# W_mix_out's product: five split weight blocks kept from the first token group for the second

## The chip, the cores and the metric

One core of one Trainium2 chip runs the kernel. The metric is the device time of one launch in microseconds (us), median of the runs shown. Every figure below is of this core.

## The reference

One layer of an encoder for 1024 tokens of width 1024, in float32. Three sub-layers follow each other, each between two RMS norms; the change lies in the end of the second one:

```
x = x + 0.5 * post1(SwiGLU_1(pre1(x)))
u = pre_mix(x)
y_ret, y_na, gates = ...                              # from u @ W_mix_in: retention, neighbourhood attention
m = sigmoid(gate_ret) * y_ret + sigmoid(gate_na) * y_na
x = x + post_mix(m @ W_mix_out)                       # W_mix_out: 1024 x 1024
x = x + 0.5 * post2(SwiGLU_2(pre2(x)))
```

## The kernel before, in words

**Split products.** TensorE multiplies in a rounded float32 (`fp32r`). Each operand is therefore split: ScalarE casts the high part h (`split`, line 60, rows "CAST"), VectorE subtracts it from the source for the rest l (line 61). A product is three matmuls, h·h, h·l, l·h (`mm3`, lines 87 to 89).

**The stage.** `out_proj` multiplies m, transposed, by W_mix_out, here `wmo`: eight blocks of 128 rows (k = 0 to 7). Left of the product stands m of one k for a group of tokens, right `wmo[k]` in two halves of 512 columns. There are eight tiles of 128 tokens in three groups, (0, 1, 2), (3, 4, 5) and (6, 7), called here the first, second and third. A group of three holds two of the six PSUM banks `ps` for each token tile. A group goes through its k one by one, for all its tokens; its last three k (`tail=3`) are held together and gone through token tile by token tile, so that the first tile is done early and its epilogue can begin. In the trace a step of one matmul of 512 columns takes 0.227 us, so one k of a group of three, 18 matmuls, takes 4.1 us.

**Weights.** `load_w` loads `wmo[k]` (512 KB) with a DMA of SyncE's queue into `wraw` (four buffers) and splits it into two pairs of pieces, rings `wh` and `wl` of nine buffers each: four and a half blocks. Each of the three groups loads and splits all eight blocks again.

**Left side.** `stream` loads m of one k for the tokens of the group (`graw`, two buffers, SyncE's queue) and splits it into `gh` and `gl` (three buffers each). m comes from the stage before, which keeps it in tiles of the pool `ro` and stores each of them to DRAM by GpSimd's queue (`store`, line 67; rows "m<-m"). The pool ends with the stage, and its memory goes on to the pool `a2`.

**Epilogue of a token tile** (`Ep.__call__`): ScalarE squares the two banks with a sum (line 219), the inverse root is taken (`rstd`, line 97, GpSimd), VectorE scales and adds the residual (lines 226 and 228), the sum is stored, normed again (line 117) and transposed on TensorE (line 126, lagging by some products) into `wx`, an object of `Winograd`. That one builds the factors of X for the next product, the third sub-layer's, in 14 buffers of tag "x" of `a2`; some come only late in this stage.

**Order.** Each engine works through its own list in order. The lists are not those of the program's text: a scheduler with a model of the times places every instruction, and a load is placed once its buffer is free by that model. A wait in front of a list holds back whatever is behind it, whether it needs that or not.

The split, the two other places that the steps below name:

```
            nc.scalar.copy(h, src)                                    # L60
            (eng or nc.vector).tensor_tensor(l, src, hf, ALU.subtract)    # L61
        raw = self.wpool.tile([P, D], F32, tag="wraw", name="wraw", bufs=4)
        self.nc.sync.dma_start(raw[:, :n], src)                       # L71
```

Of the kernel before, what the change touches and what calls it, by code (L numbers as in the profile page):

```python
# [11 lines left out]
F32R = mybir.dt.float32r  # L12
# [6 lines left out]
P = 128  # L19
D = 1024  # L20
S = 1024
KT = D // P
# [15 lines left out]
class Core:  # L38
# [94 lines left out]
            ks = slice((k % 4) * P, (k % 4 + 1) * P)  # L133
            self.mm3(bank, [p[:, ks] for p in w[k // 4]], xop(k, h), k == 0, k == nk - 1)

    def out_proj(self, nk, lhs, wload, done, groups=((0, 1, 2), (3, 4, 5), (6, 7)), tail=3, lag=8, space=3):

        left = []  # L140

        def one(t, k, a, w):
            for e in [e for e in left if e[0] <= 0]:
                left.remove(e)
                f = e[1]()
                if f is not None:
                    left.append([2, f])
            for b in range(2):
                self.mm3(banks[t][b], a[t], w[b], k == 0, k == nk - 1)
            for e in left:  # L150
                e[0] -= 1

        for toks in groups:
            banks = {t: [self.bank() for _ in range(2)] for t in toks}
            tl = tail if len(toks) > 1 else 0
            for k in range(nk - tl):
                w, a = wload(k), lhs(k, toks)
                for t in toks:
                    one(t, k, a, w)
            last = [(k, lhs(k, toks), wload(k)) for k in range(nk - tl, nk)]  # L160
            for t in toks:
                for k, a, w in last:
                    one(t, k, a, w)
                f = done(t, banks[t])
                if f is not None:
                    left.append([max(lag, max([e[0] for e in left], default=-space) + space), f])
        return [f for _, f in left]
# [508 lines left out]
def stream(c, pool, src):  # L676

    def lhs(k, toks):
        n = len(toks) * P
        p0 = toks[0] * P  # L680
        raw = pool.tile([P, 384], F32, tag="graw", name="graw", bufs=2)
        h = pool.tile([P, 384], F32R, tag="gh", name="gh", bufs=3)
        l = pool.tile([P, 384], F32R, tag="gl", name="gl", bufs=3)
        c.nc.sync.dma_start(raw[:, :n], src(k)[:, p0:p0 + n])
        c.split(h[:, :n], l[:, :n], raw[:, :n])
        return {t: (h[:, j * P:(j + 1) * P], l[:, j * P:(j + 1) * P]) for j, t in enumerate(toks)}
    return lhs
# [344 lines left out]
def trunk_layer(ctx: ExitStack, tc, x, g1a, w1i, w1o, g1b, gma, wmt, wnv, wrv, logits, dtab, rope, bias,  # L1032
# [7 lines left out]
    c = Core(tc, const, wpool, psum, dram)  # L1040
# [4 lines left out]
    def dt(name, shape):  # L1045
        return dram.tile(shape, F32, name=name)
# [3 lines left out]
    x1, x2 = dt("x1", [S, D]), dt("x2", [S, D])  # L1050
    d = {
        "a21": dt("a21", [P, 4, 512]),
        "nq": dt("nq", [NHP, P, S]), "nk": dt("nk", [NHP, P, S]), "nv": dt("nv", [16, 64, 512]), "nvg": dt("nvg", [4, 4, P, 512]),
        "no": dt("no", [NHP, P, S]), "rq": dt("rq", [RH, P, S]), "rk": dt("rk", [RH, P, S]),
        "rv": dt("rv", [TT, P, D]), "rg": dt("rg", [8, P, S]), "ry": dt("ry", [8, P, S]),
        "sr": dt("sr", [8, P, S]), "sn": dt("sn", [8, P, S]), "z": dt("z", [8, P, S]), "m": dt("m", [8, P, S]),
    }

    def rows(a):
        return lambda t: a[t * P:(t + 1) * P, :]  # L1060
# [3 lines left out]
    def pool(stack, name, side="left"):  # L1064
        return stack.enter_context(tc.tile_pool(name=name, bufs=1, side=side))


    with tc.block(schedule_with_timeline_sim=True):
        apool = pool(right, "a1", "right")
        early = pool(right, "early", "right")  # L1070
        wx = Winograd(c, (apool,) * 3, early, (14,) * 7)
# [12 lines left out]
        with tc.tile_pool(name="fin1", bufs=1) as fp:  # L1084
# [8 lines left out]
        wx = Winograd(c, (x0pool, x1pool, spool), None, (4, 4, 2, 8, 8, 8, 8), d["a21"])  # L1093
        ep_stack, g_stack = ExitStack(), ExitStack()
        ep = pool(ep_stack, "ep1")
# [7 lines left out]
        rest = ffn_out(c, xt, [junk[:, i] for i in range(4)], q, Blocks(c, (g0, g1, g1, g1), (1, 3)), w1o, wf[0], gl[0], fo,  # L1103
                       {n: (lambda j=j: ahead.update({j: c.load_w(wnv[j])})) for j, n in enumerate((65, 66, 73))})
# [65 lines left out]
        with tc.tile_pool(name="pa", bufs=1) as pa:  # L1170
# [12 lines left out]
            for i, (_, _, f, g, fn) in enumerate(jobs):  # L1183
# [14 lines left out]
                if i == mx.held + mx.saved - 1:  # L1198
# [3 lines left out]
                    for k in range(2):  # L1202
                        raw = c.raw(d["a21"][:, 2 * k:2 * k + 2].rearrange("p k t -> p (k t)"))
# [81 lines left out]
    gs = pool(g_stack, "gs2", "right")  # L1285
    ro = pool(y_stack, "ro")
    for k in range(KT):
        raw = c.raw(d["ry"][k])
        c.split(yop[0][k // 4][:, k % 4], yop[1][k // 4][:, k % 4], raw)
    for i0 in (0, 3, 6):  # L1290
        tiles = range(i0, min(i0 + 3, 8))
        m, z, w, banks = {}, {}, {}, {}
# [28 lines left out]
    apool = pool(a_stack, "a2", "right")  # L1321
    cmb = pool(left, "cmb2")
    wx = Winograd(c, (apool,) * 3, cmb, (14,) * 7)
    with tc.tile_pool(name="ep2", bufs=1) as ep:
        rest = c.out_proj(KT, stream(c, gs, lambda k: d["m"][k]), lambda k: c.load_w(wmo[k]),
                          Ep(c, ep, gmb, g2a, False, rows(x1), rows(x2), wx.put))
        fin = Pairs(c, wx, [(w2i[i], w2i[FT + i]) for i in LeftFactors.order], 3, 3)
        places = []

        def save():  # L1330
            if not places:
                h, l, r = ([gs.tile([P, 384], F32, tag=n, name=n, bufs=b) for _ in range(b)]
                           for n, b in (("gh", 3), ("gl", 3), ("graw", 2)))
                for e in (h, l):
                    places.extend([[e[0], e[1][:, :128]], [e[1][:, 128:], e[2][:, :256]]])
                places.extend([[r[0], r[1][:, :128]], [r[1][:, 128:], h[2][:, 256:], l[2][:, 256:]]])
            return places.pop(0)

        fin.lead(save, rest)
        assert not places  # L1340
        for f in rest:
            f()
# [94 lines left out]
```

## Time and profile before

| | us |
|---|---|
| median of three runs (lowest, highest) | 2271.83 (2271.73, 2274.43) |
| the profiled execution: time | 2273.08 |
| the profiled execution: span of the trace | 2271.3 |
| busy: PE (matmuls) | 2211.0 |
| busy: VectorE (DVE) | 1699.6 |
| busy: ScalarE (ACT) | 1004.9 |
| busy: GpSimd (POOL) | 577.1 |
| product of W_mix_out in the trace: the first group's first matmul | 1515.88 |
| the next product's first matmul that waits | 1612.30 |

PE is the matmul engine, PEld its weight loads, DVE, ACT and POOL are VectorE, ScalarE and GpSimd, SP and SPq SyncE and its DMA queue. In a timeline a row gives the start, the duration, engine, line, operation, the tiles out<-in and the shape; in square brackets stand the idle time ahead of it and who ended it. Successive instructions overlap by a little in these rows, so the step from start to start is shorter than the duration. The granted clock of TensorE is 0.993 on average.

### The profile page before, as it was taken

What the parts mean: (1) busy time and instruction counts of PE and PEld (TensorE: products, weight loads), DVE (VectorE), ACT (ScalarE), POOL (GpSimd) and SP (SyncE); (2) the same over time, 40 slices, a digit from 0 to 9 for tenths busy, and PEclk for the clock granted to TensorE, in tenths of its full rate; (3) what the DMA queues carried; (4) which work ended last, traced back from release to release, by engine and by line L of the source; (5) the groups of instructions that cost most, each with busy time, mean ns of one, the idle gap of its engine ahead of it and who ended that gap; (6) DMA issues with size and microseconds to landing.
All of it is one profiled execution on the core that took longest, in us unless ns stands there. A gap on an engine that the chain in (4) does not pass through costs nothing.

```text
span 2271.3 us, 30229 instructions
## 1 busy us (share of the span) xinstructions
PE 2211.0 (97%) x10288; PEld 1837.1 (81%) x10288; DVE 1699.6 (75%) x2952; ACT 1004.9 (44%) x2117; POOL 577.1 (25%) x741
## 2 busy tenths in 40 slices
PE   6999999999999999989999999999899999999998
PEld 5888888878887878878888888887688888887886
DVE  7897777655879769869876678547989887875576
ACT  6332222344555222358876665326633322234453
POOL 3243434210332224311001222101114343421022
PEclk9999999999999999999999999999999999999999
DMA  5355555476754453357655566866535555547664
GB/s 192 105 170 184 186 183 186 165 271 199 236 176 144 149 194 111 135 196 245 206 163 170 163 218 228 296 211 213 177 114 188 195 189 176 185 139 237 198 234 151
DMA packets 162459, 424.72 MB, mean 187 GB/s; under 512 B 19776, under 2 KB 47552, under 8 KB 162240
## 3 DMA queue, kind: packets, MB, share of 16 engines
q1 hardware_dynamic: 121824, 289.07, 39.5%
q0 software_dynamic: 40480, 133.72, 15.9%
q8 instruction: 81, 1.33, 0.3%
q14 instruction: 74, 0.61, 0.1%
HBM read 303.70 MB, written 123.21 MB: 188 GB/s over the span
## 4 chain that ended last, share of the span: by engine, by line
PE 42%; issue 7%; DVE 4%; DMA 3%; ACT 2%; POOL 1%; SPq 0%; POOLq 0%; DVEq 0%; ACTq 0%
PE ps L87 13%; PE ps L89 13%; PE ps L88 13%; DMA wraw<-in_dram 1%; PE pt L88 1%; PE pt L87 1%; PE pt L89 1%; DVE wl L61 1%; POOL rstd L97 1%; DMA vraw<-rv 0%; ACT wh L60 0%; DVE x L538 0%; DMA sn<-ev 0%; DVE tmp L117 0%; DMA vraw<-nvg 0%
## 5 line engine op out<-in xcount | busy, mean ns | idle before, releaser
L61 DVE TENSOR_TENSOR wl<-wraw,wh 128x512 fp32r<-128x512 f32 x662 | 479.8, 748 | 88.2 <-ACT wh L60 86.1
L60 ACT CAST wh<-wraw 128x512 fp32r<-128x512 f32 x670 | 390.6, 618 | 244.8 <-PE ps L88 71.0
L87 PE MATMUL ps<-wh,gh 128*128 128x512 f32 x612 | 239.7, 395 | 6.9 <-ACT gh L60 6.1
L88 PE MATMUL ps<-wl,gh 128*128 128x512 f32 x612 | 240.6, 394 | 0.7 <-DVE wl L61 0.7
L89 PE MATMUL ps<-wh,gl 128*128 128x512 f32 x612 | 235.2, 395 | 2.0 <-DVE gl L61 2.0
L61 DVE TENSOR_TENSOR gl<-graw,gh 128x512 fp32r<-128x512 f32 (+2 forms) x178 | 130.4, 736 | 141.0 <-ACT gh L60 138.1
L60 ACT CAST gh<-graw 128x512 fp32r<-128x512 f32 (+2 forms) x178 | 106.5, 601 | 197.8 <-PE ps L88 83.0
L87 PEld LDWEIGHTS ps<-wh,gh 128*128 128x128 f32 x612 | 116.3, 190 | 33.9 <-ACT gh L60 7.8
L89 PEld LDWEIGHTS ps<-wh,gl 128*128 128x128 f32 x612 | 116.1, 191 | 28.3 <-DVE gl L61 4.5
L528 POOL TENSOR_TENSOR q<-q,gain 128x512 f32<-128x512 f32 x30 | 52.8, 1779 | 335.7 <-ACT junk L527 124.0
L88 PEld LDWEIGHTS ps<-wl,gh 128*128 128x128 f32 x612 | 116.3, 190 | 25.2 <-DVE wl L61 1.5
L60 ACT CAST wh<-t 128x512 fp32r<-128x512 f32 x58 | 36.1, 622 | 214.9 <-DVE t L386 214.9
L87 PE MATMUL ps<-a11h,wh 128*128 128x512 f32 x280 | 110.6, 395 | 1.5 <-ACT wh L60 1.5
L87 PE MATMUL ps<-a12h,wh 128*128 128x512 f32 x280 | 110.8, 396 | 0.7 <-ACT wh L60 0.6
L87 PE MATMUL ps<-a22h,wh 128*128 128x512 f32 x280 | 109.8, 392 | 0.0
L89 PE MATMUL ps<-a22h,wl 128*128 128x512 f32 x280 | 109.1, 390 | 0.5 <-DVE wl L61 0.5
L89 PE MATMUL ps<-a12h,wl 128*128 128x512 f32 x280 | 109.6, 391 | 0.0
L88 PE MATMUL ps<-a11l,wh 128*128 128x512 f32 x280 | 109.6, 391 | 0.0
L89 PE MATMUL ps<-a11h,wl 128*128 128x512 f32 x280 | 109.6, 391 | 0.0
L88 PE MATMUL ps<-a12l,wh 128*128 128x512 f32 x280 | 109.4, 391 | 0.0
L88 PE MATMUL ps<-a22l,wh 128*128 128x512 f32 x280 | 109.1, 390 | 0.0
L97 POOL TENSOR_TENSOR rstd<-ss,mhalf 128x1 f32<-128x1 f32 x80 | 59.4, 745 | 184.6 <-DVE ss L221 74.4
(365 smaller groups left out, 5946.1 us busy)
## 6 DMA issues: line engine op xcount, KB each, us to landing
wraw<-in_dram SPq DMA_DIRECT2D x247, 512.0 KB, 4.4
lead<-in_dram POOLq DMA_DIRECT2D x44, 256.0 KB, 3.8
g0s<-cmb POOLq DMA_DIRECT2D x44, 256.0 KB, 3.0
graw<-g0s SPq DMA_DIRECT2D x44, 256.0 KB, 2.7
wq<-in_dram POOLq DMA_DIRECT2D x44, 256.0 KB, 4.0
g1s<-cmb POOLq DMA_DIRECT2D x44, 256.0 KB, 3.6
graw<-g1s SPq DMA_DIRECT2D x44, 256.0 KB, 2.7
bt<-in_dram SPq DMA_DIRECT2D x24, 384.0 KB, 3.4
```

The source lines that it names most:

```text
L60: nc.scalar.copy(h, src)
L61: (eng or nc.vector).tensor_tensor(l, src, hf, ALU.subtract)
L87: mm(ps, a[0], b[0], start=start, stop=False, skip_group_check=more)
L88: mm(ps, a[0], b[1], start=False, stop=False, skip_group_check=more)
L89: mm(ps, a[1], b[0], start=False, stop=stop, skip_group_check=more)
L97: self.nc.gpsimd.tensor_tensor(r[:, :n], ms, self.mhalf[:, :n], ALU.pow)
L528: (eng or c.nc.gpsimd).tensor_tensor(h if out is None else out, h, self.post[:, b * 512:(b + 1) * 512], ALU.mult)
```

## The change

In the first group the blocks k = 3 to 7 are no longer split into `wh` and `wl`: they go to five tiles `wk`, of four times 512 columns (both halves, h and l), in buffers of tag "x", which X's later factors take when these five are done. They stay there. The second group takes k in the order 3, 4, 5, 6, 7, 0, 1, 2, the first five from `wk`, and loads and splits only 0, 1 and 2; these are now its tail. The third group loads all eight. Five loads of 512 KB, ten casts and ten subtractions go; the matmuls are as many as before.

```diff
-    def out_proj(self, nk, lhs, wload, done, groups=((0, 1, 2), (3, 4, 5), (6, 7)), tail=3, lag=8, space=3):
+    def out_proj(self, nk, lhs, wload, done, groups=((0, 1, 2), (3, 4, 5), (6, 7)), tail=3, lag=8, space=3, orders=()):
...
-                self.mm3(banks[t][b], a[t], w[b], k == 0, k == nk - 1)
+                self.mm3(banks[t][b], a[t], w[b], k == ends[0], k == ends[1])
...
-        for toks in groups:
+        for n, toks in enumerate(groups):
             banks = {t: [self.bank() for _ in range(2)] for t in toks}
             tl = tail if len(toks) > 1 else 0
-            for k in range(nk - tl):
+            ks = orders[n] if n < len(orders) else range(nk)
+            ends = ks[0], ks[-1]
+            for k in ks[:nk - tl]:
                 w, a = wload(k), lhs(k, toks)
                 for t in toks:
                     one(t, k, a, w)
-            last = [(k, lhs(k, toks), wload(k)) for k in range(nk - tl, nk)]
+            last = [(k, lhs(k, toks), wload(k)) for k in ks[nk - tl:]]
...
     with tc.tile_pool(name="ep2", bufs=1) as ep:
-        rest = c.out_proj(KT, stream(c, gs, lambda k: d["m"][k]), lambda k: c.load_w(wmo[k]),
-                          Ep(c, ep, gmb, g2a, False, rows(x1), rows(x2), wx.put))
+        kept, asked = {}, []
+
+        def wload(k):
+            asked.append(k)
+            if asked.count(k) == 2 and k in kept:
+                return kept.pop(k)
+            if asked.count(k) > 1 or k < 3:
+                return c.load_w(wmo[k])
+            raw = c.raw(wmo[k])
+            w = apool.tile([P, 4, 512], F32R, tag="x", name="wk", bufs=14)
+            kept[k] = [(w[:, b], w[:, 2 + b]) for b in range(2)]
+            for b in range(2):
+                c.split(*kept[k][b], raw[:, b * 512:(b + 1) * 512])
+            return kept[k]
+
+        rest = c.out_proj(KT, stream(c, gs, lambda k: d["m"][k]), wload,
+                          Ep(c, ep, gmb, g2a, False, rows(x1), rows(x2), wx.put), orders=(range(KT), (*range(3, KT), *range(3))))
```

Lines behind 150 stand two further down in the changed kernel (219 is 221, 684 is 686). The order of the instructions around the first group, on the engine that splits, ScalarE, from the last stage's end to the first epilogue. Before (`wh` is a weight piece, `gh` the left side of one k for the group, `ps` a bank):

```order
L60 CAST wh<-wraw 128x512 x8
L60 CAST gh<-graw 128x384
L60 CAST wh<-wraw 128x512 x2
L60 CAST gh<-graw 128x384
L60 CAST wh<-wraw 128x512
L219 ACTIVATE tmp,ss_15335<-ps 128x512 x2
```

The two rows "gh" and "wh x2" repeat up to the last left side, k = 7, which is followed by one more weight cast and the first epilogue. The same place after the change:

```order
L60 CAST wh<-wraw 128x512 x4
L60 CAST gh<-graw 128x384
L60 CAST wk<-wraw 128x512 x5
L60 CAST gh<-graw 128x384
L60 CAST wk<-wraw 128x512 x5
L60 CAST gh<-graw 128x384
L60 CAST wh<-wraw 128x512 x5
L60 CAST gh<-graw 128x384
L60 CAST wh<-wraw 128x512 x4
L60 CAST gh<-graw 128x384
L221 ACTIVATE tmp,ss_15320<-ps 128x512 x2
```

The ten casts of the blocks that are kept now stand as a run behind the left sides of k = 3 and 4. Behind them come, still in the first group, nine casts of pieces that belong to later groups (six for k = 0, 1, 2 of the second, three for the third), five ahead of the left side of k = 6 and four ahead of that of k = 7. Before, two weight casts stood between one left side and the next.

SyncE's queue at the same place, before (`gpost`, `gpre` and `epx` belong to the epilogue):

```order
L71 DMA wraw<-in_dram 128x1024 x3
L205 DMA gpost<-in_dram 128x1024
L209 DMA gpre<-in_dram 128x1024
L215 DMA epx<-x_100 128x1024 x2
L684 DMA graw<-m 128x384
L71 DMA wraw<-in_dram 128x1024 x2
L684 DMA graw<-m 128x384
L71 DMA wraw<-in_dram 128x1024
L684 DMA graw<-m 128x384
L71 DMA wraw<-in_dram 128x1024
```

After:

```order
L71 DMA wraw<-in_dram 128x1024 x2
L207 DMA gpost<-in_dram 128x1024
L211 DMA gpre<-in_dram 128x1024
L217 DMA epx<-x_100 128x1024 x2
L686 DMA graw<-m 128x384
L71 DMA wraw<-in_dram 128x1024 x2
L686 DMA graw<-m 128x384
L71 DMA wraw<-in_dram 128x1024 x2
L686 DMA graw<-m 128x384
L71 DMA wraw<-in_dram 128x1024 x2
```

Between two loads of the left side now stand two weight loads instead of one: the loads of later groups come earlier. TensorE's order is the same but for the names of the weights, and from the third group's first epilogue on every engine's order is that of before.

## Prediction

> **What bounds the kernel now.** I read the page's busy shares first, then the stage in slices of 20 us, then the waits ahead of TensorE's instructions there, last the lists of the engines that feed it. On the page:
>
> ```profile
> span 2271.3 us, 30229 instructions
> PE 2211.0 (97%) x10288; PEld 1837.1 (81%) x10288; DVE 1699.6 (75%) x2952; ACT 1004.9 (44%) x2117; POOL 577.1 (25%) x741
> ```
>
> TensorE is busy for 97% of the span. VectorE and ScalarE, which the change relieves, are not full on average. Whether they are late in this stage is read in slices (the columns: stretch, us, PE busy, PEld, DVE, ACT, POOL, granted clock, DMA share, GB/s):
>
> ```profile
> 1520.00:1540.00 20.00, 20.00 (x90) 16.57 (x89) 8.81 (x15) 7.39 (x16) 0.00 (x0) 1.00 0.75 253
> 1540.00:1560.00 20.00, 19.41 (x93) 15.57 (x92) 16.31 (x30) 13.97 (x36) 4.54 (x7) 1.00 0.56 184
> 1560.00:1580.00 20.00, 19.96 (x92) 16.32 (x92) 15.20 (x28) 10.35 (x24) 1.85 (x3) 1.00 0.80 266
> 1600.00:1620.00 20.00, 15.91 (x49) 11.20 (x50) 18.28 (x34) 8.44 (x17) 0.00 (x0) 0.74 0.44 126
> ```
>
> In the first group (1515.9 to 1548.5) and the second (to about 1585) TensorE is full at full clock; only 0.6 of the 60 us up to 1580 is idle. The stage's losses lie behind the second group. The waits one by one (duration, what is waited for in brackets):
>
> ```profile
> 1515.88 0.39 PE L87 MATMUL ps<-wh,gh 128*128 128x512 f32 x1
> 1549.65 0.39 PE L89 MATMUL ps<-wh,gl 128*128 128x512 f32 x1
> 1550.62 0.50 PE L87 MATMUL ps<-wh,gh 128*128 128x512 f32 x1 [0.58 <-DVE tmp L226]
> 1600.27 0.63 PE L126 MATMUL pt<-ident,tmp 128*128 128x128 f32 x4 [2.34 <-DVE tmp L117]
> 1612.30 0.50 PE L87 MATMUL ps<-a11h,wh 128*128 128x512 f32 x1 [1.54 <-ACT wh L60]
> ```
>
> The first row starts the first group; the second stands 149 matmuls later, so a matmul takes 33.77 / 149 = 0.2267 us there. The wait of 0.58 is for a bank that the first tile's epilogue still holds. The waits of 2.34 and 1.54 are the last epilogue's and the next product's.
>
> **What the removed work is worth.** Ten casts, ten subtractions and five loads go. Their durations:
>
> ```profile
> 1519.47 0.62 ACT L60 CAST wh<-wraw 128x512 fp32r<-128x512 f32 x1 [3.00 <-PE ps L89]
> 1520.00 0.51 ACT L60 CAST gh<-graw 128x384 fp32r<-128x384 f32 x1
> 1520.41 0.62 ACT L60 CAST wh<-wraw 128x512 fp32r<-128x512 f32 x1
> 1520.13 0.69 DVE L61 TENSOR_TENSOR wl<-wraw,wh 128x512 fp32r<-128x512 f32 x1 [1.56 <-ACT wh L60]
> 1520.74 0.55 DVE L61 TENSOR_TENSOR gl<-graw,gh 128x384 fp32r<-128x384 f32 x1
> 1521.21 0.68 DVE L61 TENSOR_TENSOR wl<-wraw,wh 128x512 fp32r<-128x512 f32 x1
> ```
>
> From start to start a weight cast takes 0.53, a left-side cast 0.41, a subtraction 0.61 (from 1520.13 to 1520.74) and 0.47; a subtraction begins 0.66 after its cast's start. So 10 × 0.53 = 5.3 us of ScalarE, 10 × 0.61 = 6.1 us of VectorE and 2.6 MB of traffic go. All three lie beside TensorE's full stretch: of the waits before 1580 the one of 0.58 is for an epilogue, whose own chain (squares, root, two passes of VectorE) stays. At best it shrinks away: a gain between 0 and 0.58. I take 0, since the wait runs through the root and not through a cast.
>
> The third group still loads eight blocks, and from its first epilogue on all lists stand as before. What frees the banks and engines there is the end of the second group on TensorE: both engines are waiting at that point, and the third group's last block waits for a DMA, neither of which fewer splits in the second group hastens:
>
> ```profile
> 1576.67 0.60 ACT L219 ACTIVATE tmp<-ps 128x512 f32<-128x512 f32 x1 [1.26 <-PE ps L89]
> 1578.01 0.22 DVE L221 TENSOR_SCALAR ss<-ss 128x1 f32<-128x1 f32 x1 [1.88 <-ACT tmp L219]
> 1607.78 0.62 ACT L60 CAST wh<-wraw 128x512 fp32r<-128x512 f32 x1 [3.94 <-DMA wraw<-in_dram]
> ```
>
> So I cost the stretch behind 1585 at no change. If that cover fails, 2.34 and 1.54 are what can move there.
>
> **What the moved work costs.** Here the change can lose. The tiles `wk` lie in memory that the stage before held: the pool `ro`, with its tiles of m. The first `wk` cast therefore waits, on ScalarE, for the stores of m, the last of them included. Before, nothing on ScalarE waited for it. These stores, and the weight loads, by their landing (us from issue to landing):
>
> ```profile
> 1518.26 0.53 POOL L67 DMA_DIRECT2D m<-m  x1 [10.35 <-DVE m L1315]
> m<-m POOLq DMA_DIRECT2D x1, 512.0 KB, 7.5
> m<-m POOLq DMA_DIRECT2D x2, 512.0 KB, 3.5
> wraw<-in_dram SPq DMA_DIRECT2D x247, 512.0 KB, 4.4
> wraw<-in_dram SPq DMA_DIRECT2D x1, 512.0 KB, 5.7
> graw<-m SPq DMA_DIRECT2D x5, 192.0 KB, 3.7
> ```
>
> The store of 1518.26 lands after 7.5, at 1525.8, since the loads of the gains and of the residual run beside it; two earlier stores took 3.5. Weight loads take 4.4 in the median of 247, 5.7 in a slow case in the second group (issued at 1565); the left side's in this stretch 3.7.
>
> Now the chain, link by link, in the trace's time:
>
> 1. Store lands: 1525.8. Block 3's casts at 1525.8 and 1526.3, its subtractions at 1526.5 and 1527.1, done at 1527.75. TensorE wants block 3 after 3 × 18 = 54 matmuls, at 1515.88 + 54 × 0.2267 = 1528.1. That just holds, by 0.4.
> 2. Block 7's load needs the buffer that block 3 held, and is issued at 1527.8; before, it came off the list well ahead. It lands at 1527.8 + 4.4 = 1532.2. Its casts run at 1532.2 and 1532.7, block 5's left side at 1533.3 (on the list behind them), and VectorE is through block 7 and that left side at 1534.5.
> 3. The left side's raw buffer is free then: the load of k = 7's left side is issued at 1534.55, and behind it on SyncE's queue that of the third group's block 0, at 1534.95, which lands at 1539.35. The second group's block 0 is subtracted by 1535.85, which frees the buffer for the third group's block 1: issued at 1535.9, landed at 1540.3.
> 4. ScalarE's list now has four weight casts ahead of the left side of k = 7: the last of the second group's, two of the third group's block 0 and the first of its block 1. That last one can't start before 1540.3 or so. The left side of k = 7, whose own data is there at 1534.55 + 3.7 = 1538.3, is cast at 1540.95 and subtracted from 1541.6.
> 5. TensorE wants it after 5 × 18 + 12 = 102 matmuls, at 1515.88 + 102 × 0.2267 = 1539.0 (first tile: k = 5, 6, then 7). The cast's data is ready at 1541.45, so TensorE idles 2.45; the low part `gl` follows 0.35 later than its third matmul wants it.
>
> Sum: 2.45 + 0.35 = 2.8 us of idle TensorE, in a stretch where it was full, so all of it goes to the end. Behind it the second group's blocks are split long ahead, and the first epilogue on ScalarE (L219, now 221) stands behind the same left side: it shifts with TensorE and adds nothing.
>
> The ends: if the last store lands in 3.5 as the others, links 1 to 5 come 4 us earlier, more than 2.8: no idle at all, so 0 and, with the wait of 0.58 gone, -0.6. If both loads in the chain (block 7's and the third group's) take 5.7, it is 2 × 1.3 = 2.6 more: 5.4. I take the medians, since the store's 7.5 is this trace's own value under the same neighbours.
>
> **The clock.** A gap has at times a second price. Two gaps of the same kind (the left side's cast late) stand in this trace:
>
> ```profile
> 455.92 0.50 PE L87 MATMUL ps<-wh,gh 128*128 128x512 f32 x1 [2.14 <-ACT gh L60]
> 457.64 0.39 PE L88 MATMUL ps<-wl,gh 128*128 128x512 f32 x1
> 2050.93 0.50 PE L87 MATMUL ps<-wh,gh 128*128 128x512 f32 x1 [2.52 <-ACT gh L60]
> 2051.74 0.63 PE L88 MATMUL ps<-wl,gh 128*128 128x512 f32 x1
> 2053.12 1.22 PE L89 MATMUL ps<-wh,gl 128*128 128x512 f32 x2 [0.76 <-DVE gl L61]
> 2054.14 0.63 PE L87 MATMUL ps<-wh,gh 128*128 128x512 f32 x1
> 2057.98 0.63 PE L87 MATMUL ps<-wh,gh 128*128 128x512 f32 x1
> 2058.40 0.46 PE L88 MATMUL ps<-wl,gh 128*128 128x512 f32 x1
> ```
>
> After 2.14 us matmuls stay at 0.39. After 2.52 they take 0.63 up to 2057.98: nine steps from 2054.14 in 3.84, 0.427 each. Thirteen matmuls ran so: 13 × (0.427 - 0.227) = 2.6 us. My gap of 2.45 lies between the two, nearer to the dearer. I still take none: the gap of 2050.93 had a second one of 0.76 two us behind it, and mine has 0.35.
>
> [...]
>
> **The rivals.**
>
> A, the forecast: the left side of k = 7 is late by some 1 to 4 us, clock kept: +1 to +4, the likeliest +2.8.
>
> B, the gap also halves the clock: +2.8 + 2.6 = +5.4, to +8.0 with the slow loads. It decides from a gap somewhere between 2.14 and 2.52 on. For it speaks the row at 2050.93, against it 455.92. This is the case that comes out measurably slower.
>
> C, no stall: the store lands sooner, or the loads of the third group's blocks do, by 2.8 in all. For it: earlier stores took 3.5, and in the first group the DMA engines are busy for 0.75 of the time, not 1. Against it: the queue's 7.5 was met with just the loads that stay. Time: -0.6 to +1.
>
> D, the other side, faster: with five loads less the third group's last block, for which ScalarE waits 3.94 at 1607.78, lands before TensorE wants it, and the waits of 2.34 and 1.54 at 1600 and 1612 with the clock of 0.74 in that slice break up. 20 us at 0.74 lose up to 5.2; idle and clock together could give 5 us or more. It decides if that load is issued 2 us sooner or more. Against it: its place on SyncE's queue and ahead of it the same releases by TensorE. Time: 2267.
>
> **How the numbers follow.** The profiled execution took 2273.08, 1.25 above the median; its span is 2271.3, with 1.8 outside. Against its own time A gives 2275.9; against the median, which is what will be compared, 2271.83 + 2.8 = 2274.6. About 0.2%, 4.5 us, is what a measurement of this kernel can tell from no change. Chances: A 0.42, B 0.25, C 0.28, D 0.05. A and C lie within 0.2%; B at +5.4 lies beyond it. So faster 0.05, same 0.70, slower 0.25. The range: C's lower end with some scatter, 2271.0, to B's middle, 2271.83 + 5.4 = 2277.2, with half a slow load, 2278.0. What is left out is D and the upper part of B, less than 2 in 10.
>
> **What would show it.** In the trace after: `wk` casts that wait ahead of the first for the DMA m<-m, starting near 1525.8 (link 1); block 7's load issued about 1527.8 (2); the cast ahead of the last left side of the first group waiting on wraw for some us (4); TensorE with one gap of 2 to 3 us at about 1539 ahead of an L87 matmul, released by the cast of `gh` (5); matmuls of 0.39 behind it if A, of 0.63 if B; rows of 1576 to 1612 shifted as a whole if the cover holds. I am wrong if there is no wait near 1539 (the store or the loads came sooner), if TensorE waits already at 1528 (block 3's margin of 0.4 gone), or if the waits at 1600 and 1612 change.

## The result and the profile after

Over 22 runs each, the changed kernel takes 2276.81 us and the kernel before 2273.15: a ratio of 1.0017 with a 95% interval of 1.0011 to 1.0023, some 3.9 us slower. The forecast was 2.8 us slower (2274.6, range 2271.0 to 2278.0).

The two profiled executions hide most of this: 2273.81 after against 2273.08 before. So they are compared place by place. The page of the changed kernel, first lines:

```profile
span 2271.9 us, 30161 instructions
PE 2211.2 (97%) x10288; PEld 1836.7 (81%) x10288; DVE 1694.5 (75%) x2942; ACT 999.4 (44%) x2107; POOL 576.1 (25%) x741
```

The ten casts and ten subtractions are gone (ACT 2117 to 2107 instructions, DVE 2952 to 2942), and with them 5.5 us of ScalarE's busy time and 5.1 of VectorE's. TensorE executes the same 10288 matmuls. Its slices in the stage (columns as before the change):

```profile
1520.00:1540.00 20.00, 18.35 (x80) 14.41 (x79) 11.73 (x21) 10.94 (x21) 0.00 (x0) 1.00 0.74 256
1540.00:1560.00 20.00, 18.95 (x82) 14.51 (x80) 13.74 (x26) 10.45 (x29) 4.01 (x7) 0.92 0.58 207
1560.00:1580.00 20.00, 19.96 (x93) 16.38 (x94) 9.23 (x16) 5.48 (x13) 1.38 (x3) 1.00 0.38 122
1600.00:1620.00 20.00, 14.12 (x46) 9.37 (x45) 18.26 (x33) 10.47 (x23) 1.44 (x2) 0.79 0.39 128
```

Before, the first slice was full; now it is busy for 18.35, and the clock of the second is 0.92. VectorE and ScalarE are freer in the third (9.23 and 5.48 where they had 15.20 and 10.35), where TensorE was full anyway. In the third group the picture is the old one, moved by 3 to 4 us.

Here is what TensorE waits for, and its steps (start, duration):

```profile
1514.96 0.39 PE L87 MATMUL ps<-wh,gh 128*128 128x512 f32 x1
1536.56 0.39 PE L89 MATMUL ps<-wk,gl 128*128 128x512 f32 x1
1538.55 0.50 PE L87 MATMUL ps<-wk,gh 128*128 128x512 f32 x1 [1.60 <-ACT gh L60]
1538.89 0.39 PE L88 MATMUL ps<-wk,gh 128*128 128x512 f32 x1
1539.33 0.50 PE L89 MATMUL ps<-wk,gl 128*128 128x512 f32 x1
1539.66 0.50 PE L87 MATMUL ps<-wk,gh 128*128 128x512 f32 x1
1539.96 0.63 PE L88 MATMUL ps<-wk,gh 128*128 128x512 f32 x1
1541.46 0.80 PE L87 MATMUL ps<-wk,gh 128*128 128x512 f32 x1 [0.45 <-ACT gh L60]
1543.29 0.39 PE L88 MATMUL ps<-wk,gh 128*128 128x512 f32 x1
```

The group starts at 1514.96, 0.9 sooner than in the trace of before. The two gaps stand ahead of the left sides of k = 6 and k = 7. From 1536.56 to 1543.29 are eleven steps: 6.73 us, at 0.2267 each 2.49. So 4.24 are lost: 2.05 as the two waits, 2.2 as longer steps. Of these 2.2, some 1.6 belong to the clock, which is at a half from 1539.81 to 1543.22 (last section). The other 0.6 lie ahead of it, at full clock: the four steps up to 1539.66 take 3.10, of which 0.91 is their usual length and 1.60 the wait. They are the restart behind the wait, the late low part `gl` at 1539.33 among them. And the lists that feed TensorE:

```profile
1517.35 0.53 POOL L67 DMA_DIRECT2D m<-m  x1 [10.35 <-DVE m L1317]
m<-m POOLq DMA_DIRECT2D x1, 512.0 KB, 8.2
1525.91 2.71 ACT L60 CAST wk<-wraw 128x512 fp32r<-128x512 f32 x5 [6.38 <-DMA m<-m]
1531.44 1.14 ACT L60 CAST wk<-wraw 128x512 fp32r<-128x512 f32 x2 [0.84 <-DMA wraw<-in_dram]
1534.00 1.14 ACT L60 CAST wh<-wraw 128x512 fp32r<-128x512 f32 x2 [1.01 <-DMA wraw<-in_dram]
1536.15 1.14 ACT L60 CAST wh<-wraw 128x512 fp32r<-128x512 f32 x2 [1.00 <-DMA wraw<-in_dram]
1537.46 0.62 ACT L60 CAST wh<-wraw 128x512 fp32r<-128x512 f32 x1 [0.18 <-DMA wraw<-in_dram]
1537.99 0.51 ACT L60 CAST gh<-graw 128x384 fp32r<-128x384 f32 x1
1538.40 2.60 ACT L60 CAST wh<-wraw 128x512 fp32r<-128x512 f32 x4
1540.90 0.51 ACT L60 CAST gh<-graw 128x384 fp32r<-128x384 f32 x1
```

ScalarE stands for 6.38 us ahead of the first `wk` cast, for the last store of m. Three waits for weight loads follow (1.01, 1.00, 0.18), all for blocks of later groups, and only then comes the left side of k = 6, at 1537.99. Ahead of that of k = 7 four more such casts run without a wait, for 2.60 us.

To see where time goes over the whole program, the starts of the same matmuls (the n-th of the program, of 10288) are set against each other. In every trace time is counted from the matmul that lies 15 us ahead of the first group. Later than in the kernel before (profiled executions, us; minus is sooner):

```
kernel                  second group   next product   3rd sub-layer,   3rd sub-layer,
                        (no. 7300)     (no. 7600)     no. 9300         no. 9500
changed kernel             +4.4           +4.2           +4.7             +2.1
e1 elsewhere               +0.2           -0.1           -0.2             -6.8
e5 layout only              0.0           +0.2           +0.4             -6.2
e4 third3                  +0.4           -2.7           -2.4             -4.9
e6 five and three          +1.1           -5.8           -5.8            -12.4
e11 four and four          +1.8           -8.0           -8.0            -14.6
```

The changed kernel loses its 4 us in the first group and nothing afterwards. (Only one of its 22 executions was traced, so it is not known whether each of them also lost 1.6 us to the clock.) The 2.5 us that come back in the last column are the wait near 2050: behind it the clock was halved for 6.8 us in the trace of before (2051.71 to 2058.54) and for 3.4 in that of after (2055.22 to 2058.63).

### The profile page after: what moved, and what is told of

Same layout as the page of the kernel before. It is cut to its first block, busy times and chain, and to the rows that moved or that the text cites. A ratio compares the mean times of both kernels' runs of the same rounds, so it can differ in the third digit from the quotient of the medians.

```text
span 2271.9 us, 30161 instructions
## 1 busy us (share of the span) xinstructions
PE 2211.2 (97%) x10288; PEld 1836.7 (81%) x10288; DVE 1694.5 (75%) x2942; ACT 999.4 (44%) x2107; POOL 576.1 (25%) x741
## 4 chain that ended last, share of the span: by engine, by line
PE 39%; issue 7%; DVE 5%; DMA 3%; ACT 2%; POOL 1%; SPq 0%; POOLq 0%; DVEq 0%; ACTq 0%
PE ps L87 12%; PE ps L89 12%; PE ps L88 12%; DMA wraw<-in_dram 1%; DVE wl L61 1%; PE pt L87 1%; PE pt L89 1%; PE pt L88 1%; POOL rstd L97 1%; ACT wh L60 1%; DMA graw<-g1a 0%; DMA m<-m 0%; DVE x L540 0%; DVE tmp L117 0%; DMA vraw<-nvg 0%
## 5 line engine op out<-in xcount | busy, mean ns | idle before, releaser
L61 DVE TENSOR_TENSOR wl<-wraw,wh 128x512 fp32r<-128x512 f32 x642 | 466.1, 748 | 72.9 <-ACT wh L60 70.7
L60 ACT CAST wh<-wraw 128x512 fp32r<-128x512 f32 x650 | 378.6, 618 | 215.5 <-DVE wraw L412 65.3
L61 DVE TENSOR_TENSOR gl<-graw,gh 128x512 fp32r<-128x512 f32 (+2 forms) x178 | 129.8, 732 | 150.7 <-ACT gh L60 147.6
L87 PE MATMUL ps<-wh,gh 128*128 128x512 f32 x552 | 215.5, 394 | 6.4 <-ACT gh L60 6.2
L88 PE MATMUL ps<-wl,gh 128*128 128x512 f32 x552 | 216.7, 393 | 0.7 <-DVE wl L61 0.7
L89 PE MATMUL ps<-wh,gl 128*128 128x512 f32 x552 | 212.0, 395 | 1.1 <-DVE gl L61 1.1
L87 PEld LDWEIGHTS ps<-wh,gh 128*128 128x128 f32 x552 | 104.9, 190 | 30.3 <-ACT gh L60 7.9
L89 PEld LDWEIGHTS ps<-wh,gl 128*128 128x128 f32 x552 | 104.7, 190 | 24.6 <-DVE gl L61 2.9
L88 PEld LDWEIGHTS ps<-wl,gh 128*128 128x128 f32 x552 | 104.7, 190 | 23.1 <-DVE wl L61 1.5
```

The costliest lines, as they stand in the source:

```text
L87: mm(ps, a[0], b[0], start=start, stop=False, skip_group_check=more)
L88: mm(ps, a[0], b[1], start=False, stop=False, skip_group_check=more)
L89: mm(ps, a[1], b[0], start=False, stop=stop, skip_group_check=more)
```

## The experiments

Ratios are to the kernel before, run beside each, with their 95% intervals.

**What starts the chain.** e1 puts `wk` elsewhere: the s factors of X and `wk` get a pool of their own, which falls on memory of `mix` and `y` instead of `ro`.

```diff
+    lpool = pool(left, "a2k")
     cmb = pool(left, "cmb2")
-    wx = Winograd(c, (apool,) * 3, cmb, (14,) * 7)
+    wx = Winograd(c, (apool, apool, lpool), cmb, (6,) * 3 + (8,) * 4)
...
-            w = apool.tile([P, 4, 512], F32R, tag="x", name="wk", bufs=14)
+            w = lpool.tile([P, 4, 512], F32R, tag="x", name="wk", bufs=8)
```

> The changed kernel, but the five wk tiles (and X's s factors) lie in memory of the pools mix and y, which the stage before freed by its last matmul, not in ro, whose tiles of m are still being stored. Theory (the late store starts the chain): the first wk cast no longer waits for a DMA m<-m and starts by about 1519; no gap ahead of the left sides of k = 6 and 7; the 3.7 us that the change costs are gone: 2272.5 to 2273.5 where the kernel before takes 2273.2. Rival (the casts for later groups ahead of the left side are enough by themselves): a gap of 1.5 us or more stays near 1539, 2275 to 2277. Rival (removed work is worth something once the stall is gone): 2271 or less.

It took 2269.0, ratio 0.9979 (0.9970 to 0.9988): faster than the kernel before. Its ScalarE, first `wk` casts:

```profile
1517.69 4.27 ACT L60 CAST wk<-wraw 128x512 fp32r<-128x512 f32 x8 [15.92 <-PE ps L89]
```

No wait for a store, and no gap in the first group, where TensorE is busy throughout:

```profile
1515.00:1545.00 30.00, 30.00 (x134) 24.86 (x133) 18.30 (x31) 14.11 (x28) 1.09 (x2) 1.00 0.76 272
```

By the place table it neither gains nor loses in the stage. What it gains, 6.6 us in this pair of traces and 4.8 by the ratio, it gains near 2050, half a millisecond later. So the third expectation's condition was met (under 2271) but not for its reason; e5 tells which.

e5 is the kernel before with that pool alone, nothing kept and the old order of k (the lines of `lpool` and `wx` in the diff, and `load_w` for all blocks).

> The kernel before, with nothing kept and the old order of k, but with X's s factors in a pool over mix and y, as in the run with the tiles elsewhere. Theory (the 5 us that that run gains on the kernel before come from the layout alone, in the third sub-layer, where the wait of 2.52 us ahead of a left side at 2050.93 and the half clock behind it are gone): 2268 to 2270, no such wait near 2050, and the same time as the run with tiles kept within 1 us. Rival (the removed casts, subtractions and loads are what it gained): 2273 to 2274.5.

2268.86, ratio 0.9984 (0.9975 to 0.9993), equal to e1 within the intervals. The stretch from 2040 to 2060, before and then e5:

```profile
2040.00:2060.00 20.00, 16.73 (x61) 12.77 (x60) 12.30 (x15) 5.92 (x10) 8.64 (x10) 0.83 0.74 255
```

```profile
2040.00:2060.00 20.00, 20.00 (x90) 16.57 (x89) 16.48 (x19) 8.34 (x15) 9.06 (x10) 1.00 0.75 239
```

The wait of 2.52 us and the half clock are gone: with other places for the buffers the scheduler orders SyncE's queue otherwise there (two loads of x no longer stand ahead of a load of a left side). The layout is worth this, and the 5.5 us of casts, 5.1 of subtractions and 2.6 MB that the change removes are worth nothing here that can be measured: e1 has them out, e5 in.

e12 leaves `wk` over `ro` and ScalarE's list as in the changed kernel, and takes only the cause of the late landing away: the four loads of 512 KB which SyncE issues just ahead of the last store of m (two gains, two tiles of the residual) are put on GpSimd's queue behind that store.

```diff
-        nc.sync.dma_start(self.post, post)
+        e = (nc.sync if half else nc.gpsimd).dma_start(self.post, post)
+        if not half:
+            c.tc.add_manual_dep(e.ins, c.stored, ...)
...
```

> The changed kernel, wk over ro, ScalarE's list as there; only the four loads of 512 KB that SyncE issues just ahead of the last store of m (two gains, two tiles of the residual) are issued by GpSimd behind that store. Theory (the store lands late because these loads run ahead of it, and the late landing starts the chain): the store lands in 3.5 to 5.5 us, the first wk cast starts 3 to 4 us sooner against the group's first matmul, no gap over 0.5 ahead of the left sides of k = 6 and 7: 2272.5 to 2274. Rival (the landing takes its 8 us from something else): wk within 1 us of the changed kernel's, 2276 to 2277. Rival (the loads of later groups ahead of the left side suffice): wk sooner, but a gap of 1 us or more stays.

2273.57, ratio 1.0007 (0.9998 to 1.0016). The store and the first `wk` cast:

```profile
1521.41 0.53 POOL L67 DMA_DIRECT2D m<-m  x1 [10.35 <-DVE m L1323]
m<-m POOLq DMA_DIRECT2D x1, 512.0 KB, 2.9
1524.66 2.70 ACT L60 CAST wk<-wraw 128x512 fp32r<-128x512 f32 x5 [1.07 <-DMA m<-m]
```

The store lands in 2.9 us, not 8.2; the cast waits 1.07, not 6.38; TensorE has no gap in the first group, and by its matmuls loses 0.4 us in it. (The traced execution, 2277.55, is one of the longest of the twelve; when the stage begins it is already 3.2 us behind the trace of before.) The left sides still stand behind nine casts of later groups. So that order alone costs nothing; it costs when the blocks come late.

e9 goes the other way: the last tile of m is stored twice.

```diff
             c.store(d["m"][i], m[i])
+            if i == KT - 1:
+                c.store(d["m"][i], m[i])
```

> The changed kernel, wk over ro as there, but the last tile of m is stored twice in a row, so that the last store lands later. Theory (the landing of that store sets the chain): the first wk cast starts 1 to 4 us later than in the changed kernel; block 3 has only 0.4 us of margin, so TensorE now waits for wk itself or for a left side by that much more in all: 2277.5 to 2282. Rival (the store's landing is not what binds; the lists are): 2276.8 within 0.8.

2280.84, ratio 1.0039 (1.0026 to 1.0053). The second store waits for the first, the first `wk` cast for the second, and TensorE now for `wk` itself:

```profile
1531.82 0.53 POOL L67 DMA_DIRECT2D m<-m  x1 [7.97 <-DMA m<-m]
1535.42 3.22 ACT L60 CAST wk<-wraw 128x512 fp32r<-128x512 f32 x6 [5.85 <-DMA m<-m]
1536.09 0.69 PE L87 MATMUL ps<-wk,gh 128*128 128x512 f32 x1 [2.77 <-ACT wk L60]
```

Later landing, longer stall, as the theory has it. (This trace runs 5.9 us behind that of the changed kernel when the stage begins; the cast is 3.6 us later against the group.)

e10 stores that tile in two halves, `c.store(d["m"][i][:, hs], m[i][:, hs])` for each half.

> The changed kernel, wk over ro, but the last tile of m is stored in two halves, each as soon as it is done, so that the last store is half as large. Theory: the first wk cast starts 1 to 3 us sooner and the gaps of 1.60 and 0.45 shrink to under 1 in all, below what halves the clock: 2273 to 2275. Rival (the landing is set by the loads beside it, not by the store's size): first wk cast within 0.5 us of the changed kernel's, 2276 to 2277.

A miss: 2277.94, ratio 1.0027 (1.0015 to 1.0038). Both halves were issued together, at 1518.21, and landed in 7.4 us in the median, where the whole took 8.2; the first `wk` cast came only 0.5 us sooner against the group. So the same 512 KB went out at the same time, and a smaller last store was not tested; by e12, it is the loads beside the store that delay it (8.2 us with them issued just ahead of it, 2.9 with them behind it). ScalarE's list came out otherwise too, and the gaps ahead of the left sides are 1.05 and 2.09, more than the 1.60 and 0.45 of the changed kernel: the start of the casts alone does not set them.

**What carries it to TensorE.** e2 leaves `wk` over `ro` and the loads where they are, and orders the casts of the second and third group's weights behind the first group's last left side (a dependency without a wait, on ScalarE's own list).

```diff
+                c.after = c.lhs7 if n > 1 else None
                 w = c.load_w(wmo[k])      # each cast in it: add_manual_dep(cast, c.after)
```

> The changed kernel with one ordering added: ScalarE casts the weights of the second and third group behind the first group's last left side (k = 7). The wk tiles still lie over ro. Theory (both links are needed: late start, and later groups' casts ahead of the left side): the wait for m<-m stays, near 1526, but the gaps of 1.60 and 0.45 ahead of the left sides fall to under 0.5 in all: 2273 to 2273.8. Rival (the late start alone makes the left sides late): gaps of 1.5 or more stay, 2275.5 to 2277.

2274.56, ratio 1.0006 (0.9998 to 1.0015), between the two times expected. From its ScalarE and TensorE (its lines stand one to four further down, L61 for 60, L232 for 228):

```profile
1526.97 2.71 ACT L61 CAST wk<-wraw 128x512 fp32r<-128x512 f32 x5 [6.21 <-DMA m<-m]
1538.90 3.74 ACT L61 CAST wh<-wraw 128x512 fp32r<-128x512 f32 x7
1542.55 0.59 ACT L225 ACTIVATE tmp<-ps 128x512 f32<-128x512 f32 x1
1552.72 0.50 PE L91 MATMUL ps<-wk,gh 128*128 128x512 f32 x1 [2.28 <-DVE tmp L232]
```

The late start stays (6.21), and the gaps ahead of the left sides are gone, as expected. But the seven casts, 3.7 us, now stand ahead of the first epilogue's squares, and its bank comes 2.28 us late for the second group. Part of the stall has moved on. e2 and e12 together show that two things are needed: a late first `wk` cast, and casts of other groups ahead of what TensorE wants next.

e8 keeps three blocks instead of five (k = 5, 6, 7, second group in the order 5, 6, 7, 0 to 4), still over `ro`.

> The changed kernel with three blocks kept (k = 5, 6, 7) in place of five; order of the second group 5, 6, 7, 0 to 4; places over ro as in the changed kernel. The first wk cast still stands behind the store of m, but block 5 is wanted at 1536.3 only. Theory (late start times run-ahead): the wait for m<-m stays on ScalarE, block 7's load no longer hangs on block 3's buffer by a chain of two loads, the left sides are on time or late by under 1 us: 2273 to 2275. Rival (any wk cast behind the store costs the same, since the list behind it is as long): 2276 to 2277.

2272.25, ratio 0.9995 (0.9985 to 1.0006). Its first `wk` cast is as late, 10.5 us behind the group's first matmul, but its block is wanted two k later, and no gap follows in the first group. That fits a price that lies in the slack between landing and need; it does not prove it, since four casts of `wk` fewer stand on ScalarE's list as well.

e3 is the new order of k in the second group alone (`orders=(range(KT), (*range(3, KT), *range(3)))`, all blocks loaded).

> The kernel before with nothing but the new order of k in the second group (3 to 7, then 0, 1, 2); nothing is kept, all blocks are loaded and split as before. Theory: the order is free, 2273.2 within 0.5, no gap near 1539. Rival (the order costs or gains by itself, for instance at the second group's tail): over 1 us away, up to the changed kernel's 2276.8.

2273.53, ratio 0.9999 (0.9990 to 1.0007), no gap in the first group: the order is free.

**Where keeping would pay.** e4 keeps k = 5, 6, 7 from the second group for the third, on the changed kernel's places; e7 does so with the pool of e1.

```diff
+        keep = {5: (2, 3), 6: (2, 3), 7: (2, 3)}    # k: split at the 2nd request, kept for the 3rd
...
-            if asked.count(k) == 2 and k in kept:
-                return kept.pop(k)
-            if asked.count(k) > 1 or k < 3:
+            n = asked.count(k)
+            first, last = keep.get(k, (9, 9))
+            if first < n <= last:
+                return kept[k] if n < last else kept.pop(k)
+            if n != first:
                 return c.load_w(wmo[k])
...
-    orders=(range(KT), (*range(3, KT), *range(3)))     # the end of a longer line
+    orders=((0, 1, 2, 3, 4, 5, 6, 7), (0, 1, 2, 3, 4, 5, 6, 7), (5, 6, 7, 0, 1, 2, 3, 4))
```

> Keeping moved by one group: the first group is as before, the second group splits k = 5, 6, 7 into wk, and the third takes these three first and loads and splits only the other five. Theory (splits are worth nothing where TensorE is full, and something in the third group, where VectorE is busy for 17 to 18 of 20 us and TensorE waits for it): no wait for m<-m, since the store has long landed; 6 x 0.61 = 3.7 us less of VectorE in the third group, time 2269.5 to 2272. Rival (the third group's waits are the last epilogue's chain, whatever is split): 2273 within 0.7. Rival (X's factors must now wait for the kept blocks' places, in a group that has no slack): 2274.5 or more.

> The run that keeps k = 5, 6, 7 from the second group for the third, with the s factors and wk over mix and y. Theory (its gain of 3.4 us in the third group and the layout's 5 us in the third sub-layer lie in different places and add): 2265 to 2267.5. Rival (both gains are the same thing, a half clock avoided by chance of phase): 2268.5 to 2270.

e4: 2268.65, ratio 0.9985 (0.9976 to 0.9994). e7: 2264.68, ratio 0.9967 (0.9957 to 0.9978). So the gain is there and the two add. e4's first expected sign, faster, held; its mechanism only in part: TensorE still waits, for a bank at the third group's start (2.34) and for the low part of a left side at 1614.40 (3.10), but the half clock in the third group and behind it is gone. The stage from 1585 to 1645, before and then e4:

```profile
1585.00:1645.00 60.00, 51.91 (x220) 39.66 (x219) 54.27 (x98) 39.40 (x94) 10.53 (x16) 0.91 0.57 183
```

```profile
1585.00:1645.00 60.00, 50.59 (x234) 39.23 (x233) 54.54 (x98) 39.08 (x96) 11.36 (x18) 1.00 0.46 154
```

TensorE is busy for less time and yet runs 14 matmuls more, since it is at full clock. It idles for 9.4 us where it idled for 8.1, so in this trace e4 gains by the clock alone. Why the clock held is not shown: in e7's trace the same wait, 3.12 at 1614.33, was followed by matmuls of 0.58 to 0.79 from 1615.61 to 1618.60, while behind e4's 3.10 the clock stayed at 1.00. How much of the gain is due to fewer splits, and how much to the clock, these runs do not separate.

e6 joins e1 with more: five blocks kept from the first group for the second, and its last three, k = 0, 1, 2, for the third. e11 does four and four.

> The run with the wk tiles over mix and y, and one thing more: the second group splits its last three blocks, k = 0, 1, 2, into wk too, and the third group, in its old order, takes these three and loads and splits only the other five. Theory (splits have a price only in the third group): no gap in the first group, and in the third some of the waits at 1600 and 1612 or of the half clock there goes: 2265.5 to 2268 where the tiles elsewhere alone take 2269. Rival (the waits in the third group only move): 2269 within 0.8. Rival (X's factors wait for their places): 2270 or more.

> The fastest version so far (wk and s factors over mix and y; five blocks kept from the first group for the second, three from the second for the third, 2261.1) with four and four in place of five and three: the first group keeps k = 4 to 7, the second splits 0 to 3 into wk for the third. The second group loads and splits four, the third four. Theory (each block fewer in the third group takes 1.2 us off VectorE where TensorE waits for it): 2258.5 to 2261. Rival (X's factors need the places: eight of them are now all held at the start of the third group): 2262 or more. Rival (what is left there is the epilogue's chain): 2261 within 0.7.

e6: 2261.14, ratio 0.9957 (0.9945 to 0.9970), faster than expected. e11: 2260.63, ratio 0.9951 (0.9939 to 0.9964), the fastest, but not told apart from e6: both its theory and its last rival allow this time. Its profiled stage:

```profile
1585.00:1645.00 60.00, 56.72 (x263) 44.94 (x262) 54.89 (x99) 37.48 (x93) 10.94 (x18) 1.00 0.44 145
```

43 matmuls more in these 60 us than before, at full clock throughout: what a block less to split is worth depends on the group that is spared. One thing stays open. e6 spares the third group three splits, as e7 does, and the second group five more; its median is 3.5 us lower. The intervals of the two overlap, and their orders of k differ, so whether the second group's five are worth something there is not shown.

## Why the prediction was right, point by point

**Bound and removed work: right.** It was costed at 0, and e1 against e5 bears it out: with and without these casts, subtractions and loads the matmuls of the second group come within 0.2 us of each other.

**Link 1, the store: right.** The first `wk` cast waits for m<-m; it starts 10.95 us behind the group's first matmul, where 9.9 was worked out (the store took 8.2, not 7.5). Block 3 was still in time.

**Link 2: right.** Block 7's casts start 16.5 behind the group's start, forecast 16.3.

**Links 3 to 5: right mechanism, wrong k.** The left side is late because later groups' casts wait for their loads ahead of it. I looked only at k = 7, but the five casts ahead of k = 6 are the ones that wait: the larger gap, 1.60, is there. The four ahead of k = 7 found their loads landed, ran one right behind the other and added 0.45. With the 0.6 of the restart that makes 2.65, where 2.45 and 0.35 were forecast. That the sum comes so near is in part luck: one gap was worked out, and two others came.

**The clock: the term that was mis-sized.** I took 0 and priced its loss at 2.6 in a rival. It came, with 1.6. The step that failed is the reading of the two gaps of 2.14 and 2.52 as a threshold in the length of a gap, with mine taken as free because 0.35 follows it and not 0.76. The wait of 1.60 was followed by half clock, and in the same trace one of 2.21, at 456.19, was not (last section). So the outcome, some 3.9, lies between A (2.8) and B (5.4): B's mechanism with a smaller gap and 3.4 us at half clock instead of 6.8. The range held both A and B, so that the time lies in it does not speak for A.

**Behind the second group: right.** The waits of 2.34 and 1.54, and the third group's last block, in the changed kernel:

```profile
1603.98 0.63 PE L126 MATMUL pt<-ident,tmp 128*128 128x128 f32 x4 [2.56 <-DVE tmp L117]
1615.43 0.50 PE L87 MATMUL ps<-a11h,wh 128*128 128x512 f32 x1 [1.04 <-ACT wh L60]
1610.91 0.62 ACT L60 CAST wh<-wraw 128x512 fp32r<-128x512 f32 x1 [3.36 <-DMA wraw<-in_dram]
```

2.56 and 1.04, and 3.36 where it was 3.94: the same three waits, the one at 1612 shorter by 0.5; the delay is 4.4 us ahead of them and 4.2 behind. Rival D did not happen here; something like it did in e4 and e11, which spare the third group itself.

**Rival C** (the store lands sooner) is what e12 made true: no stall, 1.0007.

## What to carry to other kernels

Before a tile is put into memory that another stage frees, look up what that stage does last with it: a store that was still landing became a wait of 6.38 us ahead of the new tile's first cast here, and TensorE waited 1.60 and 0.45 us for left sides behind it on ScalarE's list. Work taken off an engine that is not late where it is taken off was worth nothing here (e1 against e5), however many microseconds it was: choose the stage first, then the work. And where a change of a few us moves memory, run the new layout without the change; here the layout alone gained some 4 us (e5), as much as the change lost.

## What the runs showed of the hardware

**Waits of one length were followed by full clock at one place and by half at another.** The trace of before at its two gaps (2.14 at 455.92 and 2.52 at 2050.93), then that of after at the two of its first group (1.60 at 1538.55 and 0.45 at 1541.46), in rows as long as the time at half clock there, 3.41 us (columns as above; the eighth figure, behind POOL's, is the clock):

```profile
454.27:457.68 3.41, 1.76 (x8) 1.43 (x8) 1.78 (x1) 2.43 (x5) 3.39 (x5) 1.00 1.05 380
457.68:461.10 3.42, 2.90 (x13) 2.13 (x12) 3.42 (x4) 0.89 (x2) 3.07 (x5) 1.00 0.95 331
...
2048.30:2051.71 3.41, 0.90 (x4) 0.67 (x4) 1.49 (x2) 2.00 (x4) 3.40 (x4) 1.00 1.01 378
2051.71:2055.12 3.41, 2.65 (x7) 1.61 (x6) 3.41 (x3) 0.21 (x1) 3.39 (x5) 0.50 0.84 306
2055.12:2058.54 3.42, 3.42 (x10) 2.65 (x9) 1.29 (x3) 1.14 (x2) 0.73 (x2) 0.50 0.87 295
```

```profile
1536.39:1539.81 3.42, 1.77 (x7) 0.87 (x6) 2.99 (x6) 3.11 (x7) 0.00 (x0) 1.00 0.93 368
1539.81:1543.22 3.41, 2.96 (x8) 1.76 (x7) 2.38 (x5) 1.58 (x4) 0.00 (x0) 0.50 0.78 246
1543.22:1546.63 3.41, 3.41 (x16) 2.81 (x16) 1.22 (x3) 1.30 (x4) 0.56 (x1) 1.00 0.84 330
```

The clock is at a half from 2051.71 to 2058.54 before, 6.8 us, and from 1539.81 to 1543.22 after, 3.4 us. The length of the wait alone does not tell the cases apart. In the trace of after a wait of 2.21 at 456.19 was followed by full clock, one of 2.18 at 2054.34 and that of 1.60 at 1538.55 by 3.4 us at half. In e8's trace the wait near 2050, 2.29 at 2051.26, was followed by matmuls of 0.39 to 0.40. Nor does the idle time in these rows: TensorE is idle for 1.65 us from 454.27 before and for 1.65 from 1536.39 after, with full clock behind the first and half behind the second. In the rows at half clock it is idle for 0.76 from 2051.71, with half behind it, and for 0.45 from 1539.81, with full. What decides it is not shown.

**The store of m landed in 8.2 us behind four loads and in 2.9 ahead of them.** The same 512 KB, stored by GpSimd's queue, landed in 8.2 us with four loads of that size issued just ahead by SyncE's queue (after), and in 2.9 with these issued behind it on its own queue (e12).
